# Attention in pairs of heads, with P times V as two fp32 products in the two column halves of TensorE's array and row sums by adds

## The chip, the cores and the metric

The kernel runs on one core of one Trainium2 chip. The metric is the device time of one execution in microseconds, the median of several runs. Three runs of the kernel before gave 4182.15, 4182.94 and 4184.15 us.

## What is computed

Two layers of a hybrid backbone over 256 context tokens and 2,048 latent tokens, 1,024 wide. In each layer one projection feeds three kinds of heads: a bidirectional state-space scan (6 heads), a bidirectional gated DeltaNet (4 heads) and attention (6 query heads, 2 key/value heads of 64 columns). Their outputs are joined and projected back. The change is in the attention:

```python
def _attend(q, k, v):
    ...
    def block(qi):
        s = jnp.einsum('bqhgd,bkhd->bhgqk', qi, k).astype(jnp.float32) * scale
        pr = jax.nn.softmax(s, axis=-1).astype(v.dtype)
        return jnp.einsum('bhgqk,bkhd->bqhgd', pr, v)
```

All is fp32. Head h uses key/value head h // 3. The context tokens attend to themselves in layer 0; in layer 1, the last, only the 2,048 latent tokens are wanted.

## The kernel before

TensorE multiplies in two formats here. `fp32` products are exact enough by themselves; `fp32r` products round their operands, so where precision matters a number is split into a rounded part and a rest, and several fp32r products are added. In the trace an fp32 product leaves two records, an fp32r product one.

Each layer has three parts: the projection, the mixers, the output projection. The mixers run interleaved: DeltaNet preparation (`gdn_pre`, `gdn_solve`), state-space scan (`ssd_states`, `ssd_out`), then the DeltaNet chain (`gdn_chain`), 18 steps of two half steps that each need the one before: products L1094, L1104 and L1114 with copies between them. Attention is written around it as a generator, `attention()`: its first 8 pieces are taken before the chain is written, the rest after. The order on each engine is not that of the text. A scheduler sorts all instructions of the program into one queue per engine by their dependences and its own estimate of their times, so attention fills what the other mixers leave.

Attention is tiled in units. A unit is one head and 512 query columns (24 units in a layer, and 6 small ones of 256 columns in layer 0), over 18 key tiles of 128 rows.

- `unit_max` loads the unit's queries (q2, by DMA on SP's queue; qm, a copy by GpSimd, L522), computes scores for 20 pieces of keys (pq, L531), reduces each to row maxima on VectorE (L533), and turns the negative maxima into a row of qm by four fp32 products with the identity (pm, L541) and a VectorE copy (L542).
- `unit_main` computes for each key tile the transposed scores minus the maximum (pst) by two fp32r products (L562 with khh, L563 with klo and qm), lets ScalarE take the exponential (pe, L565), and multiplies by V into po (L556). V has a column of ones between its two heads (v1, 129 columns), so the product has 65 rows, 64 of values and one of row sums.
- The first 13 units of a layer do this as one fp32 product per key tile. The last 11 split: ScalarE rounds pe to ph (L570), VectorE subtracts to pl (L571), and three fp32r products of ph and pl with the parts of V (vh) replace the fp32 one.
- At a unit's end ScalarE copies po out (L579), and two DMAs store the row sums and the values.

PSUM's eight banks: three for scores (ps_s), one for po, one that every fourth score tile may use before the chain (ps_x), three for the other mixers (four during the chain).

```python
ops = [(v1, pe)] if ph is None else [(vh[0], ph), (vh[1], ph), (vh[0], pl)]
...
nc.tensor.matmul(pst[g * 64:g * 64 + 64, d * 192:(d + 1) * 192], bn[:, g * 64:g * 64 + 64],
                 xd[:, d, 3 * g:3 * g + 3, :], start=True, stop=True)
```

The last two lines are L789 in `ssd_states`: products of 64 output rows that go into the two halves of the partitions in turn. Such a product uses 64 of the array's columns; the trace writes it as 128*64.

## Time and profile before

| | us |
|---|---|
| median of three runs | 4182.94 |
| span of the profiled execution | 4198.6 |
| TensorE busy | 4005.7 (95%) |
| VectorE busy | 2858.0 (68%) |
| ScalarE busy | 1834.2 (44%) |
| GpSimd busy | 1500.3 (36%) |

The profiled execution has no time of its own beside its span, from the first to the last instruction; durations below are its. The attention of layer 0 lies between 711 and 1902 us, that of layer 1 between 2795 and 3991; the rest is projection and output projection. Records of TensorE are longer than the time that a product holds the array, since the next one starts before the last has ended: what a product costs is read from where the next one starts.

### The profile page before, as it was taken

The page shows a single profiled execution, that of the slowest core. Times are in us where ns is not written, and L with a number is a line of the kernel's source. Part 1 is how long each engine was busy: PE and PEld are TensorE (multiplying, and loading weights), DVE is VectorE, ACT ScalarE, POOL GpSimd, SP SyncE. Part 2 cuts the span into 40 slices and gives each one's busy share as a digit, 9 for nine tenths or more (in the row PEclk, how much of TensorE's full clock was granted, in tenths as well). Part 3 has the DMA queues.
Part 4 walks back from the last instruction along what each step waited for, and adds up shares of the span by engine and source line. Part 5 has one row for each costly group of instructions (what it writes and reads, how often), then busy time and mean ns, then how long its engine had stood idle before and what let it go on. Part 6 is the DMA issues. An engine that isn't in the chain of part 4 may idle for free. (4 is left out here: it accounts for less than half of the span.)

```text
span 4198.6 us, 66336 instructions
## 1 busy us (share of the span) xinstructions
PE 4005.7 (95%) x23574; PEld 3044.2 (73%) x23574; DVE 2858.0 (68%) x5652; ACT 1834.2 (44%) x3817; POOL 1500.3 (36%) x1854
## 2 busy tenths in 40 slices
PE   7999999999999999998899999999999999999989
PEld 5899998554566667776678999985545666666667
DVE  6556564889876667875546665648898757677643
ACT  5343432443565545653224434324335645555610
POOL 5121120676465323432313211206755632234300
PEclk9999999999999889999999999999999989898999
DMA  6343432344123333426743434323541233434254
GB/s 198 109 137 103 129 111 93 111 149 165 51 60 89 88 80 83 108 64 214 224 161 118 148 102 128 113 93 103 165 136 55 59 82 77 87 81 97 53 171 155
DMA packets 539143, 477.46 MB, mean 114 GB/s; under 512 B 113784, under 2 KB 476732, under 8 KB 538812
## 3 DMA queue, kind: packets, MB, share of 16 engines
q1 hardware_dynamic: 496956, 437.81, 36.3%
q10 hardware_dynamic: 41856, 35.40, 2.8%
q8 instruction: 187, 3.06, 0.3%
q14 instruction: 144, 1.18, 0.1%
HBM read 328.91 MB, written 144.18 MB: 113 GB/s over the span
## 5 line engine op out<-in xcount | busy, mean ns | idle before, releaser
L565 ACT ACTIVATE pe<-pst 128x512 f32<-128x512 f32 (+1 forms) x876 | 511.7, 594 | 713.7 <-PE pst L563 690.2
L533 DVE TENSOR_REDUCE mx<-pq 128x1 f32<-128x512 f32 (+1 forms) x972 | 594.4, 626 | 135.2 <-PE pq L531 130.8
L531 PE MATMUL pq<-khh,q 128*128 128x512 f32 (+1 forms) x972 | 473.9, 512 | 26.7 <-DVE mx L533 24.8
L556 PE MATMUL po<-pe,v 128*65 128x512 f32 x960 | 487.8, 597 | 1.1 <-ACT os__12118 L579 1.0
L562 PE MATMUL pst<-q,khh 128*128 128x512 f32 (+1 forms) x876 | 433.5, 495 | 16.9 <-DVE mx L533 15.8
L455 PE MATMUL ps<-lo,wh 128*128 128x384 f32 (+2 forms) x1296 | 441.2, 340 | 0.0
L455 PE MATMUL ps<-hi,wl 128*128 128x384 f32 (+2 forms) x1296 | 441.0, 340 | 0.0
L455 PE MATMUL ps<-hi,wh 128*128 128x384 f32 (+2 forms) x1296 | 440.9, 340 | 0.0
L563 PE MATMUL pst<-qm,klo 65*128 65x512 f32 (+1 forms) x876 | 359.1, 411 | 0.0
L401 PE MATMUL ps<-wh,hi 128*128 128x320 f32 (+1 forms) x1120 | 354.3, 318 | 1.9 <-DVE hi L365 1.8
L571 DVE TENSOR_TENSOR pl<-pe,ph 128x512 fp32r<-128x512 f32 x396 | 301.2, 765 | 76.4 <-ACT ph L570 58.6
L401 PE MATMUL ps<-wl,hi 128*128 128x320 f32 (+1 forms) x1120 | 350.3, 314 | 0.0
L401 PE MATMUL ps<-wh,lo 128*128 128x320 f32 (+1 forms) x1120 | 349.7, 315 | 0.7 <-DVE lo L366 0.7
L531 PEld LDWEIGHTS pq<-khh,q 128*128 128x128 f32 x972 | 190.1, 198 | 176.6 <-issue 65.1
L376 DVE TENSOR_TENSOR wl<-wt,wh 128x1024 fp32r<-128x1024 f32 (+3 forms) x144 | 175.8, 1250 | 159.5 <-ACT wh L375 159.3
L556 PE MATMUL po<-ph,vh 128*65 128x512 f32 x792 | 274.7, 429 | 0.6 <-ACT ph L570 0.6
L562 PEld LDWEIGHTS pst<-q,khh 128*128 128x128 f32 x876 | 172.9, 197 | 127.1 <-issue 53.3
L570 ACT CAST ph<-pe 128x512 fp32r<-128x512 f32 x396 | 242.6, 619 | 47.0 <-PE po L556 22.1
L455 PEld LDWEIGHTS ps<-lo,wh 128*128 128x128 f32 x1296 | 244.0, 188 | 10.7 <-issue 0.4
L455 PEld LDWEIGHTS ps<-hi,wl 128*128 128x128 f32 x1296 | 243.4, 188 | 10.4
L455 PEld LDWEIGHTS ps<-hi,wh 128*128 128x128 f32 x1296 | 243.5, 188 | 10.2
L1044 POOL TENSOR_TENSOR wb<-cst,dsc 64x512 f32<-64x512 f32 x72 | 92.8, 1289 | 423.6 <-issue 225.1
(585 smaller groups left out, 8849.4 us busy)
## 6 DMA issues: line engine op xcount, KB each, us to landing
wt<-in_w_in_dram SPq DMA_DIRECT2D x72, 512.0 KB
acv<-pre_d SPq DMA_DIRECT2D x68, 512.0 KB
wmt<-in_w_mod_dram SPq DMA_DIRECT2D x48, 512.0 KB
pre_d<-pre SPq DMA_DIRECT2D x34, 512.0 KB
kqc<-kt_d SPq DMA_DIRECT2D x68, 256.0 KB
wt<-in_w_in_dram SPq DMA_DIRECT2D x24, 668.0 KB
wt<-in_w_in_dram SPq DMA_DIRECT2D x24, 640.0 KB
q<-qt_d SPq DMA_DIRECT2D x48, 256.0 KB
```

What stands on the lines that cost most here:

```text
L376: nc.vector.tensor_tensor(out=wl[:, ks, :], in0=wt, in1=wh[:, ks, :].bitcast(F32), op=ALU.subtract)
L401: nc.tensor.matmul(ps, hh[:, k, a], ww[:, k, :], start=(n == 0), stop=(n == 3 * KD - 1))
L455: nc.tensor.matmul(ps, ww[:, k, m * P:(m + 1) * P], hh[:, k, s0:s0 + sn], start=(n == 0), stop=(n == 3 * KD - 1))
L531: nc.tensor.matmul(pq[:, :n], q2[:, u * P:(u + 1) * P], khh[:, kvh, k0t * P + a:k0t * P + a + n], start=True, stop=True)
L533: nc.vector.tensor_reduce(mx[:, i:i + 1], pq[:, :n], axis=AX.X, op=ALU.max)
L556: nc.tensor.matmul(po[0:65, :qn], v[:, kt, vs], p[:, :qn], start=(kt == k0t and j == 0), stop=(kt == k1t - 1 and j == len(ops) - 1))
L562: nc.tensor.matmul(pt[:, :qn], khh[:, kvh, ks], q2[:, :qn], start=True, stop=False)
L563: nc.tensor.matmul(pt[:, :qn], klo[:, kvh, ks], qm[:, :qn], start=False, stop=True)
L565: nc.scalar.activation(out=pe[:, :qn], in_=pt[:, :qn], func=AF.Exp, scale=0.125)
L570: nc.scalar.copy(out=ph, in_=pe)
L571: nc.vector.tensor_tensor(out=pl, in0=pe, in1=ph.bitcast(F32), op=ALU.subtract)
L1044: nc.gpsimd.tensor_tensor(out=wb[dk[d], d, :, :, cS[d]].rearrange("p c h n -> p (c h) n"), in0=cc("ident")[dk[d], None, dk[d]].to_broadcas ...
```

## The change

Units become pairs of heads: 12 of 512 columns in a layer, 3 small ones in layer 0. `v1` loses its column of ones. For each key tile the scores of both heads go into one `pe` of 1,024 columns (five buffers, before four of 512), and P times V is one fp32 product per head, 64 rows each, into partitions 0 to 63 and 64 to 127 of po. No unit splits the exponentials any more. Row sums are made apart, in a bank pl of their own: in the first four pairs of a layer and in the small ones ("P") by fp32 products with a matrix of ones, also in halves; in the other eight pairs GpSimd ("G", 14 of 18 tiles) and VectorE ("V", 4 of 18) add the tiles up, and two products per engine and pair finish the sum. P times V runs three tiles behind the scores, two tiles at a time. The maxima are turned by fp32r products of 65 rows and copied by ScalarE; qm's other rows come by DMA. ps_x is gone, pl takes its bank, and the chain has three banks instead of four. Four pieces of attention, each of two heads, are written before the chain.

```diff
-        v1 = kv.tile([P, NT, 129], F32, name="v1")
+        v1 = kv.tile([P, NT, P], F32, name="v1")
...
-                    if g == 0 and bi == 3:
-                        nc.gpsimd.tensor_copy(v1[:, :, 64:65], cc("ones")[:, None, 0:1].to_broadcast([P, NT, 1]))
...
-                                    nc.vector.tensor_copy(v1[:, t, 0:64], ps[:, 192:256])
-                                    nc.vector.tensor_copy(v1[:, t, 65:129], ps[:, 256:320])
+                                    nc.vector.tensor_copy(v1[:, t, :], ps[:, 192:320])
...
-                psg[2] += 1
-                if psg[0] and psg[2] > 60 and psg[2] % 4 == 0:
-                    return psg[0].tile([P, 512], F32, name=name, tag="x")
                 return ps_s.tile([P, 512], F32, name=name, tag="s")
 
-            banks(1, 3)
-
-            def unit_max(h, q0, qn, k0t, k1t, st):
-                kvh = h // 3
-                q2 = ap_.tile([P, 512], F32R, name="q2", bufs=3)
+            banks(0, 3)
+
+            nmz = apz.tile([P, 2, 4, 65], F32R, name="nmz")
+            nc.gpsimd.memset(nmz.bitcast(F32), 0.0)
+
+            def unit_max(pr, q0, qn, k0t, k1t, st):
+                h0, nu = 2 * pr, qn // P
+                q2 = ap_.tile([P, 2, 512], F32R, name="q2", bufs=3)
+                qm = ap_.tile([65, 2, 512], F32R, name="qm", bufs=3)
                 with tc.high_priority():
-                    nc.sync.dma_start(q2[:, :qn].bitcast(F32), qt_d[:, h, q0:q0 + qn])
-                qm = ap_.tile([65, 512], F32R, name="qm", bufs=3)
-                nc.gpsimd.tensor_copy(qm[0:64, :qn], q2[0:64, :qn].bitcast(F32))
+                    nc.sync.dma_start(q2[:, :, :qn].bitcast(F32), qt_d[:, h0:h0 + 2, q0:q0 + qn])
+                    nc.sync.dma_start(qm[0:64, :, :qn].bitcast(F32), qt_d[0:64, h0:h0 + 2, q0:q0 + qn])
                 st.update(q2=q2, qm=qm)
                 kn = (k1t - k0t) * P
                 pieces = [(a, min(512, kn - a)) for a in range(0, kn, 512)]
-                nm = ap_.tile([P, 4], F32, name="nm")
-                for u in range(qn // P):
-                    mx = ap_.tile([P, 8], F32, name="mx", bufs=4)
-                    for i, (a, n) in enumerate(pieces):
-                        pq = aslot("pq")
-                        nc.tensor.matmul(pq[:, :n], q2[:, u * P:(u + 1) * P], khh[:, kvh, k0t * P + a:k0t * P + a + n],
-                                         start=True, stop=True)
-                        nc.vector.tensor_reduce(mx[:, i:i + 1], pq[:, :n], axis=AX.X, op=ALU.max)
-                        yield
-                    nc.vector.tensor_reduce(nm[:, u:u + 1], mx[:, 0:len(pieces)], axis=AX.X, op=ALU.max)
-                nc.vector.tensor_scalar(out=nm[:, :qn // P], in0=nm[:, :qn // P], scalar1=-1.0, scalar2=None, op0=ALU.mult)
+                mx = ap_.tile([P, 2, 4, 5], F32, name="mx")
+                for j in range(2):
+                    kvh = (h0 + j) // 3
+                    for u in range(nu):
+                        for i, (a, n) in enumerate(pieces):
+                            pq = aslot("pq")
+                            nc.tensor.matmul(pq[:, :n], q2[:, j, u * P:(u + 1) * P], khh[:, kvh, k0t * P + a:k0t * P + a + n],
+                                             start=True, stop=True)
+                            nc.vector.tensor_reduce(mx[:, j, u, i:i + 1], pq[:, :n], axis=AX.X, op=ALU.max)
+                            yield
+                for j in range(2):
+                    nc.vector.tensor_reduce(nmz[:, j, 0:nu, 64:65], mx[:, j, 0:nu, 0:len(pieces)], axis=AX.X, op=ALU.max, negate=True)
                 for _ in range(3):
                     yield
-                pm = aslot("pm")
-                for u in range(qn // P):
-                    nc.tensor.matmul(pm[64:65, u * P:(u + 1) * P], nm[:, u:u + 1], ident, start=True, stop=True)
-                nc.vector.tensor_copy(qm[64:65, :qn], pm[64:65, :qn])
+                for j in range(2):
+                    pm = aslot("pm")
+                    for u in range(nu):
+                        nc.tensor.matmul(pm[0:65, u * P:(u + 1) * P], nmz[:, j, u, :], identr, start=True, stop=True)
+                    nc.scalar.copy(out=qm[64:65, j, :qn], in_=pm[64:65, :qn])
                 yield
 
-            def unit_main(h, q0, qn, k0t, k1t, st, sp=()):
-                kvh = h // 3
+            def unit_main(pr, q0, qn, k0t, k1t, st, how):
+                h0 = 2 * pr
+                kvh = (h0 // 3, (h0 + 1) // 3)
                 q2, qm = st["q2"], st["qm"]
                 po = ps_o.tile([P, 512], F32, name="po", tag="po")
-                pend = []
+                pl = ps_o.tile([P, 512], F32, name="pl", tag="pl")
+                ones = cc("ones")[:, 0:64]
+                half = (slice(0, 64), slice(64, 128))
+                pend, held, acc = [], {}, {}
+                plan = [how(kt - k0t) for kt in range(k0t, k1t)]
+                n_pl = plan.count("P") + len({e for e in plan if e != "P"})
+                done = [0]
+
+                def sums(src):
+                    for j in range(2):
+                        nc.tensor.matmul(pl[half[j], :qn], ones, src[:, j, :qn], start=(done[0] == 0), stop=(done[0] == n_pl - 1))
+                    done[0] += 1
 
                 def pv():
-                    kt, pe, ph, pl = pend.pop(0)
-                    vs = slice(kvh * 64, kvh * 64 + 65)
-                    ops = [(v1, pe)] if ph is None else [(vh[0], ph), (vh[1], ph), (vh[0], pl)]
-                    for j, (v, p) in enumerate(ops):
-                        nc.tensor.matmul(po[0:65, :qn], v[:, kt, vs], p[:, :qn], start=(kt == k0t and j == 0),
-                                         stop=(kt == k1t - 1 and j == len(ops) - 1))
+                    kt, pe = pend.pop(0)
+                    for j in range(2):
+                        nc.tensor.matmul(po[half[j], :qn], v1[:, kt, kvh[j] * 64:kvh[j] * 64 + 64], pe[:, j, :qn],
+                                         start=(kt == k0t), stop=(kt == k1t - 1))
+                    if plan[kt - k0t] == "P":
+                        sums(pe)
 
                 for kt in range(k0t, k1t):
                     ks = slice(kt * P, (kt + 1) * P)
-                    pt = aslot("pst")
-                    nc.tensor.matmul(pt[:, :qn], khh[:, kvh, ks], q2[:, :qn], start=True, stop=False)
-                    nc.tensor.matmul(pt[:, :qn], klo[:, kvh, ks], qm[:, :qn], start=False, stop=True)
-                    pe = ap_.tile([P, 512], F32, name="pe", bufs=4)
-                    nc.scalar.activation(out=pe[:, :qn], in_=pt[:, :qn], func=AF.Exp, scale=0.125)
-                    ph = pl = None
-                    if kt in sp:
-                        ph = spl.tile([P, 512], F32R, name="ph", bufs=2)
-                        pl = spl.tile([P, 512], F32R, name="pl", bufs=2)
-                        nc.scalar.copy(out=ph, in_=pe)
-                        nc.vector.tensor_tensor(out=pl, in0=pe, in1=ph.bitcast(F32), op=ALU.subtract)
-                    pend.append((kt, pe, ph, pl))
-                    if len(pend) > (3 if sp else 1):
+                    pe = ap_.tile([P, 2, 512], F32, name="pe", bufs=5)
+                    for j in range(2):
+                        pt = aslot("pst")
+                        nc.tensor.matmul(pt[:, :qn], khh[:, kvh[j], ks], q2[:, j, :qn], start=True, stop=False)
+                        nc.tensor.matmul(pt[:, :qn], klo[:, kvh[j], ks], qm[:, j, :qn], start=False, stop=True)
+                        nc.scalar.activation(out=pe[:, j, :qn], in_=pt[:, :qn], func=AF.Exp, scale=0.125)
+                    e = plan[kt - k0t]
+                    if e != "P":
+                        eng = nc.gpsimd if e == "G" else nc.vector
+                        if e in acc:
+                            eng.tensor_tensor(out=acc[e][:, :, :qn], in0=acc[e][:, :, :qn], in1=pe[:, :, :qn], op=ALU.add)
+                        elif e in held:
+                            acc[e] = ap_.tile([P, 2, 512], F32, name="acc" + e, bufs=1)
+                            eng.tensor_tensor(out=acc[e][:, :, :qn], in0=held[e][:, :, :qn], in1=pe[:, :, :qn], op=ALU.add)
+                        else:
+                            held[e] = pe
+                    pend.append((kt, pe))
+                    if len(pend) >= 4:
+                        pv()
                         pv()
                     yield
                 while pend:
                     pv()
-                os_ = ap_.tile([65, 512], F32, name="os_", bufs=1)
-                nc.scalar.copy(out=os_[:, :qn], in_=po[0:65, :qn])
-                ob, sb_ = (0, 64) if kvh == 0 else (1, 0)
-                nc.sync.dma_start(sm_d[None, HQ * q0 + h * qn:HQ * q0 + (h + 1) * qn], os_[sb_:sb_ + 1, :qn])
-                nc.sync.dma_start(mx_d[640 + h * 64:704 + h * 64, q0:q0 + qn], os_[ob:ob + 64, :qn])
+                for e in held:
+                    sums(acc.get(e, held[e]))
+                os_ = ap_.tile([P, 512], F32, name="os_", bufs=1)
+                nc.scalar.copy(out=os_[:, :qn], in_=po[:, :qn])
+                sm_ = ap_.tile([65, 512], F32, name="sm_", bufs=1)
+                nc.scalar.copy(out=sm_[:, :qn], in_=pl[0:65, :qn])
+                for j in range(2):
+                    f0 = HQ * q0 + (h0 + j) * qn
+                    nc.sync.dma_start(sm_d[None, f0:f0 + qn], sm_[64 * j:64 * j + 1, :qn])
+                nc.sync.dma_start(mx_d[640 + h0 * 64:768 + h0 * 64, q0:q0 + qn], os_[:, :qn])
                 yield
...
+                def early(k):
+                    return "P"
+
+                def late(k):
+                    return "V" if k % 4 == 3 else "G"
...
-                    if i == 13:
-                        for _ in range(2):
-                            vh.append(spl.tile([P, NT, 129], F32R, name=f"vh{len(vh)}", bufs=1))
-                        nc.scalar.copy(out=vh[0], in_=v1)
-                        nc.vector.tensor_tensor(out=vh[1], in0=v1, in1=vh[0].bitcast(F32), op=ALU.subtract)
-                    spn = () if i < 13 else range(NT)
                     nxt = ms[i:i + 1] + mb[i + 1:i + 2]
-                    left = (21 + 3) * (i + 1 < len(big)) + 3 * (i < len(small))
+                    left = 43 * (i + 1 < len(big)) + 7 * (i < len(small))
                     done = 0
-                    for j, _ in enumerate(unit_main(*un, sb[i], spn)):
-                        want = left * (j + 1) // (NT - 4)
+                    for j, _ in enumerate(unit_main(*un, sb[i], early if i < 4 else late)):
+                        want = left * (j + 1) // (NT - 2)
                         adv(nxt, want - done)
                         done = max(done, want)
                     adv(nxt, 99)
                     if i < len(small):
-                        for _ in unit_main(*small[i], ss_[i]):
+                        for _ in unit_main(*small[i], ss_[i], early):
                             pass
-                    if i >= 14:
-                        next(side_work, None)
...
-            for _ in range(8):
+            for _ in range(4):
                 next(att)
-            banks(0, 4)
+            banks(0, 3)
             gdn_chain(rq)
```

The scheduler sorts the queues anew. Two places on TensorE's queue show what becomes of the pairs; the rows name product and operands (pq scores for the maxima, pst transposed scores, po the output, pl the sums; the size is that of the output).

In layer 0, beside the DeltaNet preparation, the kernel before (L556 is P times V, L531 the scores for the maxima):

```order
L556 MATMUL po_11202<-pe_11258,v1_352 65x512
L531 MATMUL pq_11273<-khh_350,q2_11246 128x512
L531 MATMUL pq_11276<-khh_350,q2_11246 128x256
L556 MATMUL po_11202<-pe_11270,v1_352 65x512
L531 MATMUL pq_11287<-khh_350,q2_11246 128x512
L934 MATMUL ptv_7374<-cst_63,kv__7318 128x128
```

The same stage of the changed kernel (L564 is P times V, L558 the sums, L528 the scores for the maxima, L969 DeltaNet preparation):

```order
L528 MATMUL pq_11139<-khh_350,q2_11067 128x512
L564 MATMUL po_11011<-pe_11119,v1_352 64x512
L558 MATMUL pl_11012<-pe_11119,cst_63 64x512
L969 MATMUL pg_7597<-kq_7529 64x128 x4
L969 MATMUL pg_7604<-kq_7529 64x128 x4
L528 MATMUL pq_11142<-khh_350,q2_11067 128x256
L564 MATMUL po_11011<-pe_11119,v1_352 64x512
L558 MATMUL pl_11012<-pe_11119,cst_63 64x512
```

The two halves that read one pe no longer follow each other: between L564 and L558 of the first head and those of the second stand products of other shapes, and each L558 follows the L564 of its own half.

In layer 0, beside the chain, the kernel before, with a split head (L556 three times per tile, L562 and L563 transposed scores):

```order
L556 MATMUL po_18197<-ph_18304,vh0_16670 65x512
L556 MATMUL po_18197<-ph_18304,vh1_16671 65x512
L531 MATMUL pq_18331<-khh_350,q2_18207 128x512
L562 MATMUL pst_18334<-q2_17900,khh_350 128x512
L563 MATMUL pst_18334<-qm_17902,klo_351 128x512
L531 MATMUL pq_18346<-khh_350,q2_18207 128x512
L556 MATMUL po_18197<-pl_18305,vh0_16670 65x512
L556 MATMUL po_18197<-ph_18324,vh0_16670 65x512
L556 MATMUL po_18197<-ph_18324,vh1_16671 65x512
```

The changed kernel beside the chain (L1116, L1126 and L1090 are chain and its preparation, L574 and L575 transposed scores):

```order
L564 MATMUL po_17929<-pe_17951,v1_352 64x512
L1116 MATMUL p_13937<-Z0_13855,kqc_13726 64x64 x4
L564 MATMUL po_17929<-pe_17951,v1_352 64x512
L1090 MATMUL pv_13897<-xf0_12743,vt_13914 32x32 x16
L1116 MATMUL p_13937<-Z1_13860,kqc_13726 64x64 x4
L574 MATMUL pst_17976<-q2_17560,khh_350 128x512
L575 MATMUL pst_17976<-qm_17561,klo_351 128x512
L528 MATMUL pq_17981<-khh_350,q2_17940 128x512
L564 MATMUL po_17929<-pe_17971,v1_352 64x512
L528 MATMUL pq_17984<-khh_350,q2_17940 128x512
L1126 MATMUL p_13950<-r0_13946,xf1_12744 64x64 x4
```

Here too one product of the chain or of the scores stands between the two L564 of one pe.

## Rows read from the trace of the kernel before

**Rows 1.** Page, sections 1 and 2: busy time of TensorE; its granted clock in 40 slices.

```profile
PE 4005.7 (95%) x23574; PEld 3044.2 (73%) x23574; DVE 2858.0 (68%) x5652; ACT 1834.2 (44%) x3817; POOL 1500.3 (36%) x1854
PEclk9999999999999889999999999999999989898999
```

**Rows 2.** Windows of the attention, layer 0 then 1, before and beside the chain.

```profile
core 0: us, PE busy (x) PEld busy (x) DVE busy (x) ACT busy (x) POOL busy (x), PEclk, DMA share, GB/s
711.00:1340.00 629.00, 594.09 (x2766) 345.37 (x2765) 520.59 (x1144) 297.52 (x739) 389.53 (x510) 0.99 0.34 102
1340.00:1902.00 562.00, 542.40 (x4166) 393.54 (x4163) 403.37 (x758) 311.79 (x609) 198.04 (x170) 0.91 0.38 87
2795.00:3395.00 600.00, 571.42 (x2661) 339.30 (x2660) 497.44 (x1095) 278.77 (x680) 362.23 (x472) 0.98 0.32 99
3395.00:3991.00 596.00, 565.46 (x4225) 403.93 (x4222) 407.04 (x758) 317.11 (x618) 187.13 (x172) 0.89 0.38 81
```

**Rows 3.** Groups by shape: TensorE, VectorE, ScalarE and GpSimd (busy, mean | idle before).

```profile
L556 PE MATMUL po<-pe,v 128*65 128x512 f32 x936 | 481.5, 603 | 1.1 <-ACT os__12118 L579 1.0
L556 PE MATMUL po<-ph,vh 128*65 128x512 f32 x792 | 274.7, 429 | 0.6 <-ACT ph L570 0.6
L541 PE MATMUL pm<-cst,nm 128*1 128x128 f32 x408 | 56.6, 283 | 5.1 <-DVE nm L536 3.5 <-DVE zn L420 1.6
L571 DVE TENSOR_TENSOR pl<-pe,ph 128x512 fp32r<-128x512 f32 x396 | 301.2, 765 | 76.4 <-ACT ph L570 58.6 <-PE po L556 13.0 <-ACT Z L1106 1.7
L565 ACT ACTIVATE pe<-pst 128x512 f32<-128x512 f32 x864 | 507.5, 597 | 710.6 <-PE pst L563 687.3 <-PE po L556 15.2 <-DVE pl L571 1.2
L217 POOL TENSOR_TENSOR wml<-wmt,wmh 128x1024 fp32r<-128x1024 f32 x24 | 62.9, 2636 | 55.3 <-ACT wmh L214 55.1
L981 POOL TENSOR_TENSOR M<-N,B 128x1024 f32<-128x1024 f32 x4 | 8.0, 1990 | 14.4 <-DMA B<-be_d 7.4 <-DMA cd_d<-pre 7.0
```

**Rows 4.** Timeline of TensorE, whole heads with fp32 P times V: start, length, instructions.

```profile
1005.90 1.02 PE L556 MATMUL po<-pe,v 128*65 128x512 f32 x2
1006.36 1.03 PE L531 MATMUL pq<-khh,q 128*128 128x512 f32 x2
1007.23 0.39 PE L562 MATMUL pst<-q,khh 128*128 128x512 f32 x1
```

**Rows 5.** Timeline of TensorE, head with split exponentials.

```profile
1671.64 0.40 PE L556 MATMUL po<-pl,vh 128*65 128x512 f32 x1
1671.87 0.62 PE L556 MATMUL po<-ph,vh 128*65 128x512 f32 x2
1672.33 0.40 PE L562 MATMUL pst<-q,khh 128*128 128x512 f32 x1
```

**Rows 6.** Timeline of TensorE where the used part of the array changes.

```profile
1642.32 0.50 PE L562 MATMUL pst<-q,khh 128*128 128x512 f32 x1
1642.66 0.41 PE L563 MATMUL pst<-qm,klo 65*128 65x512 f32 x1
...
1655.20 0.39 PE L563 MATMUL pst<-qm,klo 65*128 65x512 f32 x1
1655.52 0.96 PE L1104 MATMUL p<-r,xf 64*64 64x64 f32 x16
```

**Rows 7.** Timeline of TensorE, products of 192 columns: four records, then two.

```profile
1001.42 0.55 PE L789 MATMUL pst<-xd,bn 128*64 128x192 f32 x4
1001.89 0.64 PE L556 MATMUL po<-pe,v 128*65 128x512 f32 x1
...
3233.39 0.49 PE L843 MATMUL po<-S,bc 64*128 64x192 f32 x2
3233.81 0.44 PE L835 MATMUL pd<-rr,sufr 128*128 128x384 f32 x1
```

**Rows 8.** Waits of TensorE, 711 to 1340 us.

```profile
PE pst L562 <- DVE mx L533: 10.2, 13, 2.1
PE pq L531 <- DVE mx L533: 8.7, 9, 3.7
```

14 lines of the change are left out of this document (8 added, 6 removed).

## The prediction

> **What bounds the kernel now.** I read the page first: TensorE is busy for 95% of the span, and its clock is granted nearly whole [rows 1]. Then the windows, to see the stages that the change touches. In both layers attention runs in two stretches: beside the state-space and DeltaNet preparation (711 to 1340 us, 2795 to 3395), then beside the DeltaNet chain (1340 to 1902, 3395 to 3991). TensorE is busy for 94 to 97% of each, VectorE for at most 83%, ScalarE for 55%, GpSimd for 62% [rows 2]. So what counts is TensorE's time. Busy time is no price, since records overlap (a mean of 603 ns for one of the two records of an fp32 product [rows 3]). I price by starts in the timeline.
>
> - An fp32 product of 512 columns: from 1005.90 to 1007.23 stand one product P times V (two records) and two fp32r products. An fp32r product takes 0.23 us (1671.64 to 1671.87 [rows 5]). 1.33 - 0.47 = **0.86 us** [rows 4].
> - A split tile: 0.46 us for two products and 0.23 for the third, **0.70 us** [rows 5]. Nearly the price of one fp32 product, so giving up the split gains little by itself.
>
> The change must therefore win by running two fp32 products in one product's time. Do column halves overlap? The kernel has such a place: L789 puts products of 192 columns alternately into the halves. Four records, two products, take 0.47 us until the next line starts; the two records of one product of that length take 0.42 [rows 7]. So two halves **that follow each other directly** do run side by side. Whether they follow each other is the order's to say.
>
> **The change, part by part.**
>
> *P times V and row sums.* On TensorE's queue the changed kernel has 876 half-width products at L564 and 364 at L558, 1,240 in all, 24 of them 256 columns wide. The pairs are written next to each other, but the queue has them apart: pst and pq products, 128 columns wide, stand between the halves. I counted along the queue how many products find the other half as direct neighbour: 90. So 1,150 turns of the array remain where 620 were meant. At 0.86 us: 989, less 24 x 0.43 = 10 for the narrow ones: 979 us. Before: 468 wide fp32 products x 0.86 and 12 narrow ones x 0.43 make 408 us, 396 split tiles x 0.70 make 277. **+294 us.** A lone half costs as much as a whole array: the rate per column is the same for 192 columns in a half, above, as for 512 of 65.
>
> *Changes of the used part.* Between a product that uses 128 columns and one that uses 64 the array does not stream on. Going in takes 0.32 us where 0.23 is normal (1655.20 to 1655.52 [rows 6]): 0.09. The first wide product after a narrow stretch takes 0.34 (1642.32 to 1642.66): 0.10 more. Inside and on leaving: two passes of 192 columns stream for 0.86 x 192/512 = 0.32 us, and L789 takes 0.47 to 0.48: 0.16 more [rows 7]. 0.35 for a visit, or 0.17 for one change. Both queues have many already, in the chain's 64x64 products and in L541's single-column ones. Counted along the queues by shape, there are 1,242 changes before and 2,445 after; 1,203 x 0.17 = **+205 us.**
>
> *The row of maxima.* L541's 204 fp32 products of 128 columns (408 records [rows 3]) become fp32r at L539: 204 x 0.86 x 128/512 = 44 us become 204 x 0.23/4 = 12. **-32 us.** Scores and maxima (L562, L563, L531) keep their numbers: 0.
>
> Sum on TensorE: 294 + 205 - 32 = **+467 us** at full clock. Most of it falls in the stretches beside the preparation, which were granted 0.98 and 0.99, a little beside the chain (0.91 and 0.89) [rows 2]; at 0.97 it is 481.
>
> *What stops covering.* TensorE waited 19 us in the first stretch for VectorE to empty a slot [rows 8]. With TensorE slower, VectorE is ahead; I take back 15 us a layer, **-30**. Against it, attention now ends before the chain: 144 of the chain's 576 first products (L1116) stand behind the last attention row, 18 of its 72 half steps. A half step takes 562/36 = 15.6 us now [rows 2], with attention in it: 1,177 fp32r products and 40 rows of maxima stand on the queue in that stretch, 279 us, 307 at its clock. That leaves 7.1 us for a half step's own products, changes and waits. Alone it may wait for its copies where attention filled in: between 0 and 8.5 us more for each of 18. I take 1.8, near the low end because the 7.1 already hold waits, **+32**; the ends are 0 and +153.
>
> *Other engines, at nothing.* 396 casts leave ScalarE and 396 subtractions (765 ns) VectorE [rows 3]; neither bounds, so that gains nothing beyond the 30 above. 16 late pairs bring 13 adds each to GpSimd and 3 to VectorE. No GpSimd add of 128x1024 fp32 is in the trace; the nearest are 1,990 and 2,636 ns [rows 3], so 26 to 34 us a pair. The same pair holds TensorE for 72 x 0.23 (scores) + 40 x 0.23 (maxima) + 40 x 0.86, 60 us even without changes, and GpSimd is 62% busy at most: covered, if its queue does not come late. VectorE's 48 adds cost less than its 396 subtractions did. ScalarE's new copies (two maxima rows, one more result per pair) are some 0.6 us each on an engine half idle. The qm rows come by DMA instead of GpSimd: 27 more transfers on SP's queue, with a DMA share of 0.32 to 0.38. One PSUM bank less for scores early, three instead of four for the chain: 0, with an upper bound of some 20 us a layer, doubling the waits of [rows 8]. v1's copies in the projection: two become one, off the path.
>
> Together 481 - 30 + 32 = **+483 us**. The profiled span, 4198.6 us, becomes 4682; it stands 15.7 above the median of the plain runs, so I say 4183 + 483, some **4665 us**.
>
> **The rivals.**
>
> *Changes cost nothing (chance 0.12).* A narrow product of 512 columns may hide the weight load and emptying that products of 64 and 192 show. For it: my price comes from short products. Against it: the first wide product after is 512 long and still takes 0.34 [rows 6]. Then 262/0.97 - 30 + 32 = +272: **4455 us**.
>
> *The clock falls (0.12).* Beside the chain, where narrow products and waits are many, 0.89 to 0.91 was granted, not 0.98 [rows 2]; that is stretches at 1.2 instead of 2.4 GHz. Now the earlier stretches are full of narrow products too. They grow to some 1,830 us for both layers; at 0.90 that is 9% more, +165: **4830 us**. Against it: fp32 products of 65 columns held 0.99 before.
>
> *GpSimd holds the exponentials (0.08).* pe has five buffers, and one is free only when the add has read it. GpSimd's queue is in order; an add behind the chain's weight products, or behind a wait for a DMA, comes late, exp waits for a buffer and TensorE for exp. One such hold of 6 us, three adds, in each of 16 pairs: +100, **4765 us**. It decides as soon as GpSimd falls more than four tiles behind.
>
> *The halves overlap after all (0.06): faster.* The mechanism is that halves of a pair share one turn of the array although other products stand between them in the queue. Then 620 turns: 533 - 5 = 528, against 685 now, and 32 saved: -189 us. With the changes at half price, -86; with the clock and the chain's tail, -90: **4095 us**. It needs more than some 540 of the 620 pairs to overlap before it pays for the changes. For it: L789's halves overlap [rows 7]. Against it: they are neighbours in the queue, and here 90 are. The Trainium skill, page TensorEngine Tiling (Array Packing), section Theoretical Speedup, speaks for it: a dimension of at most 64 gives up to twice the speed, and by that alone P times V and the sums would take the 528 us. The Trainium skill, page TensorE: Matmul & The Clock Gate, Part 3, speaks against it: products start and end in program order, with no reordering. No row here shows a half overlapping across a wide product.
>
> **How the numbers follow.** 0.62 for the forecast as priced, 0.12 + 0.12 + 0.08 for the slower rivals, 0.06 for the faster one. The range goes from the case without a price for changes to the case with the lower clock and some of the tail's upper bound: **4455 to 4870 us**, which leaves out the faster case and about a seventh of the rest. Faster by over 0.2% (what a measurement of this kernel can tell from no change, some 8 us) 0.06, within it 0.01, slower 0.93.
>
> **What would show it.** Right: L564 groups of one or two records with pst and pq between them, 0.86 us apart from their neighbour's start plus the change; the stretch before the chain longer by some 300 us a layer, since 926 of the 1,240 half products stand ahead of the chain, the one beside it shorter by some 40; TensorE the busy engine in both; the end of attention before the chain's end. Wrong: L564 rows of both halves with nearly the same start throughout; or long waits of TensorE for exp with GpSimd busy; or a chain tail of over 100 us a layer. If L564 stands alone but its visit takes well under 1.2 us, the price of a change was wrong.

## The result and the profile after

| | before | after |
|---|---|---|
| median, us | 4183.55 (4 runs) | 4680.95 (4 runs, 4678.85 to 4684.12) |
| span of the profiled execution, us | 4198.6 | 4678.6 |
| TensorE busy, us | 4005.7 | 4481.5 |
| mean granted clock | 0.958 | 0.954 |

The changed kernel is slower: its time is 1.1165 times that of before, 95% interval 1.1121 to 1.1208. The forecast was 4665 us. The span grew by 480.0 us and TensorE's busy time by 475.8, so the loss is TensorE's, as [rows 1] had it. The page of the changed kernel, busy time and granted clock:

```profile
PE 4481.5 (96%) x23702; PEld 2983.3 (64%) x23702; DVE 2658.6 (57%) x5008; ACT 1616.5 (35%) x3473; POOL 1939.6 (41%) x2008
...
PEclk9999998999999999976999999989999999999679
```

Its groups by shape, P times V and the sums (busy us, mean ns of a record | idle before), beside [rows 3]:

```profile
L564 PE MATMUL po<-pe,v 128*64 128x512 f32 x1728 | 886.5, 626 | 0.0
...
L558 PE MATMUL pl<-pe,cst 128*64 128x512 f32 x576 | 288.4, 593 | 0.0
```

The other engines lie well below TensorE. The clock is low in the slices in which the chain runs alone at the end of each layer's mixers. The same stages as in [rows 2], as windows (columns: window, length, busy time of PE, PEld, DVE, ACT, POOL, granted clock, DMA share, GB/s). For each layer: first transposed score to first chain product, then to the last P times V, then to the end of the chain.

```profile
738.00:1643.00 905.00, 887.96 (x3416) 403.68 (x3415) 568.67 (x1119) 336.15 (x804) 507.10 (x541) 0.99 0.25 73
1643.00:2020.00 377.00, 375.98 (x2716) 210.82 (x2715) 186.48 (x308) 132.61 (x280) 221.76 (x139) 0.99 0.38 85
2020.00:2163.00 143.00, 115.28 (x866) 91.62 (x867) 71.66 (x131) 40.56 (x83) 86.46 (x75) 0.56 0.66 169
...
3091.00:3954.00 863.00, 849.12 (x3232) 382.01 (x3234) 541.21 (x1055) 314.90 (x737) 478.89 (x517) 0.99 0.24 70
3954.00:4347.00 393.00, 392.03 (x2782) 216.22 (x2781) 186.29 (x311) 134.83 (x283) 224.81 (x138) 0.97 0.36 82
4347.00:4469.00 122.00, 93.71 (x784) 83.69 (x783) 49.84 (x109) 26.72 (x67) 61.40 (x63) 0.55 0.47 109
```

Where the 480 us lie, with the same marks in both traces (the start is that of the kernel, in layer 1 the end of layer 0's mixers; the mixers end with the last product of attention or chain):

| | layer 0 | layer 1 |
|---|---|---|
| start to the first transposed score | +29 | +25 |
| to the first chain product | +263 | +258 |
| to the end of the mixers | -35 | -62 |

The two layers sum to 478, and the output projection adds the rest. The loss sits in the stretch ahead of the chain, where TensorE is busy for 888 of 905 us. Beside the chain the time fell although TensorE was busier than before. Behind the last P times V the chain has 143 and 122 us left, at about half the clock; behind the last row sum, which ends at 2034.3 and 4367.2 us, it runs alone for 129 and 102. The last row sum of layer 0 and the first of the ten half steps behind it:

```profile
2032.42 1.92 PE L558 MATMUL pl<-accV,cst 128*64 128x512 f32 x4
...
2039.99 1.28 PE L1116 MATMUL p<-Z,kqc 64*64 64x64 f32 x13
```

What one visit of the array's half costs is in the timeline (start, length, instruction):

```profile
1008.84 1.07 PE L564 MATMUL po<-pe,v 128*64 128x512 f32 x2
1009.75 1.02 PE L558 MATMUL pl<-pe,cst 128*64 128x512 f32 x2
1010.70 0.50 PE L528 MATMUL pq<-khh,q 128*128 128x512 f32 x1
1011.13 0.64 PE L564 MATMUL po<-pe,v 128*64 128x512 f32 x1
```

A half product, a half product of sums and one wide fp32r product take from 1008.84 to 1011.13, 2.29 us. At the plain rates of 0.86, 0.86 and 0.23 they would take 1.95. The visit costs 0.34 us more, the prediction's two changes at 0.17. Both half products belong to one head and so to the same half of the array; the other head's follow behind wide products.

### The profile page after: what moved, and what is told of

It is laid out like the page before. It is cut to its first block, busy times and chain, and to the rows that moved or that the text cites. A ratio compares the mean times of both kernels' runs of the same rounds, so it can differ in the third digit from the quotient of the medians.

```text
span 4678.6 us, 65132 instructions
## 1 busy us (share of the span) xinstructions
PE 4481.5 (96%) x23702; PEld 2983.3 (64%) x23702; DVE 2658.6 (57%) x5008; ACT 1616.5 (35%) x3473; POOL 1939.6 (41%) x2008
## 5 line engine op out<-in xcount | busy, mean ns | idle before, releaser
L564 PE MATMUL po<-pe,v 128*64 128x512 f32 x1752 | 892.1, 622 | 0.0
L576 ACT ACTIVATE pe<-pst 128x512 f32<-128x512 f32 x876 | 496.2, 593 | 1069.5 <-PE pst L575 1063.1
L581 POOL TENSOR_TENSOR accG<-accG,pe 128x1024 f32<-128x1024 f32 x192 | 459.6, 2394 | 263.4 <-ACT pe L576 261.1
L528 PE MATMUL pq<-khh,q 128*128 128x512 f32 (+1 forms) x972 | 407.2, 455 | 25.8 <-DVE mx L530 12.3
L574 PE MATMUL pst<-q,khh 128*128 128x512 f32 x876 | 405.2, 463 | 15.9 <-DVE mx L530 14.0
L574 PEld LDWEIGHTS pst<-q,khh 128*128 128x128 f32 x876 | 165.6, 189 | 328.0 <-issue 106.8
L528 PEld LDWEIGHTS pq<-khh,q 128*128 128x128 f32 x972 | 181.6, 197 | 297.5 <-issue 106.3
L575 PE MATMUL pst<-qm,klo 65*128 65x512 f32 x876 | 347.4, 397 | 0.0
L564 PEld LDWEIGHTS po<-pe,v 128*64 128x64 f32 x1752 | 161.0, 136 | 230.8 <-issue 211.5
L558 PE MATMUL pl<-pe,cst 128*64 128x512 f32 x600 | 293.8, 585 | 0.0
L1245 PE MATMUL psd<-woh,mh 128*128 128x512 f32 x544 | 215.5, 398 | 31.2 <-ACT mh L1236 29.0
```

The lines of the kernel that those rows point to most:

```text
L528: nc.tensor.matmul(pq[:, :n], q2[:, j, u * P:(u + 1) * P], khh[:, kvh, k0t * P + a:k0t * P + a + n], start=True, stop=True)
L558: nc.tensor.matmul(pl[half[j], :qn], ones, src[:, j, :qn], start=(done[0] == 0), stop=(done[0] == n_pl - 1))
L564: nc.tensor.matmul(po[half[j], :qn], v1[:, kt, kvh[j] * 64:kvh[j] * 64 + 64], pe[:, j, :qn], start=(kt == k0t), stop=(kt == k1t - 1))
L574: nc.tensor.matmul(pt[:, :qn], khh[:, kvh[j], ks], q2[:, j, :qn], start=True, stop=False)
L575: nc.tensor.matmul(pt[:, :qn], klo[:, kvh[j], ks], qm[:, j, :qn], start=False, stop=True)
L576: nc.scalar.activation(out=pe[:, j, :qn], in_=pt[:, :qn], func=AF.Exp, scale=0.125)
```

## The experiments

Twelve kernels ran. Two theories were put first. **A**: TensorE's work adds up wherever it stands. **B**: beside the chain the chain keeps a pace of its own, so only work ahead of it counts.

### e1_pairs: the two halves as direct neighbours

```diff
+ def pair(mm):
+     mm(1)
+     with tc.high_priority():
+         tc.keep_in_program_order(mm(0))
- for j in range(2):
-     nc.tensor.matmul(po[half[j], :qn], ...)
+ pair(lambda j: nc.tensor.matmul(po[half[j], :qn], ...))
```

The sums (pl) are issued in the same way.

> The second product of each pair is tied to the place right behind the first, nothing else changes. On TensorE's queue 1,240 half products then take 620 turns instead of 1,150, and the used part of the array changes 1,783 times instead of 2,445. Theory A (TensorE's work adds up in both stretches, as the prediction had it): 530 x 0.86 + 662 x 0.17 = 569 us less, 4112 us, faster than the kernel before. Theory B (beside the chain the pace is the chain's own, 14 to 15 us for a half step with or without attention, so only what stands ahead of the chain counts): ahead of the chain 882 turns become 458 and 1,499 changes 1,017, 365 + 82 = 447 us less, 4234 us. Rival C (halves overlap anyway, or the loss has another cause): 4680 us, no change.

Measured: 4405.13 us (ratio to before 1.0502, 1.0458 to 1.0547), 276 less than the changed kernel. The timeline shows two products, four records, where one stood:

```profile
1008.68 1.08 PE L568 MATMUL po<-pe,v 128*64 128x512 f32 x4
1009.59 1.03 PE L563 MATMUL pl<-pe,cst 128*64 128x512 f32 x4
1010.55 0.50 PE L578 MATMUL pst<-q,khh 128*128 128x512 f32 x1
```

From 1008.68 to 1009.59 are 0.91 us for two halves; above, 0.91 us held one. Halves overlap here when they are direct neighbours; with other products between them each held the array for a time of its own. In the groups the products of P times V and the sums fall from 886.5 + 288.4 to these:

```profile
L568 PE MATMUL po<-pe,v 128*64 128x512 f32 x1728 | 513.7, 676 | 0.2 <-ACT pe L580 0.2
...
L563 PE MATMUL pl<-pe,cst 128*64 128x512 f32 x576 | 152.1, 607 | 0.3 <-ACT sm__11894 L603 0.3
```

That is 509 us less, and still only 276 are gained. The prices hold roughly: busy time multiplied by the mean granted clock, a rough measure of the work, fell by some 528 us (4481.5 x 0.954 less 4122.2 x 0.909), near the 569 of theory A. Two things keep the time from following. The windows, cut at the same three marks (layer 0):

```profile
741.00:1530.00 789.00, 727.05 (x3416) 373.90 (x3415) 585.62 (x1121) 340.30 (x806) 502.88 (x540) 0.94 0.28 83
1530.00:1890.00 360.00, 352.79 (x2603) 223.24 (x2599) 181.05 (x298) 130.12 (x270) 216.03 (x134) 0.85 0.37 85
1890.00:2041.00 151.00, 123.60 (x985) 98.95 (x984) 71.24 (x140) 44.12 (x91) 92.45 (x82) 0.57 0.69 175
```

First, the chain's stretch did not shorten: 360 + 151 = 511 us against 377 + 143 = 520, as B says. Ahead of it 116 us are gained. Second, the granted clock fell, from 0.99 to 0.94 ahead and 0.85 beside. TensorE is idle for 62 us of the 789, mostly waiting for VectorE's maxima, where it was idle for 17 of 905. One place where the clock falls (in brackets the idle time before):

```profile
1134.26 0.50 PE L578 MATMUL pst<-q,khh 128*128 128x512 f32 x1
1134.60 0.40 PE L579 MATMUL pst<-qm,klo 65*128 65x512 f32 x1
1137.17 0.79 PE L578 MATMUL pst<-q,khh 128*128 128x512 f32 x1 [2.16 <-DVE mx L530]
1137.76 0.63 PE L579 MATMUL pst<-qm,klo 65*128 65x512 f32 x1
```

Before the wait the step from L578 to L579 takes 0.34 us, behind it 0.59: the engine is at 1.2 GHz, here until about 1161. B's direction holds, its amount does not: both theories left the clock at its height.

### e2_later, e3_all_late, e4_early_start: the same work elsewhere

e2 holds the maxima of the sixth and later units back until the chain's first product (a dependence of order alone); e3 takes the row sums of all large pairs by adds; e4 gives q2 and mx tiles of their own, allocated ahead of the others.

```diff
# e2_later, in unit_max
+ if gated and j + u + i == 0:
+     behind(mm)
...
# e3_all_late, in attention
- unit_main(*un, sb[i], early if i < 4 else late)
+ unit_main(*un, sb[i], late)
# e4_early_start, in unit_max
- q2 = ap_.tile([P, 2, 512], F32R, name="q2", bufs=3)
+ q2 = apq.tile([P, 2, 512], F32R, name="q2", bufs=3)
...
```

> The changed kernel, halves apart as they are (1,162 turns, 2,464 changes), but the sixth pair of each layer and those after it may not start before the chain's first product. It only moves attention: ahead of the chain 584 turns are left of 882, 840 changes of 1,499 and 1,020 score products of 1,945; behind the chain now stand 230 turns, 434 changes and 600 score products. Theory A: the work is the same, only the chain's lonely end goes, 4640 to 4660 us. Theory B: 256 + 112 + 213 = 581 us less ahead, 198 + 74 + 138 = 410 more behind, up to 80 more beside the chain: 4510 to 4590 us.

> All large pairs sum their rows by adds on GpSimd and VectorE; 256 products of the sums go (1,150 turns become 900, 2,445 changes 2,289). The scheduler then puts all attention of a layer ahead of the chain (1,945 score products there become 2,724, changes 1,499 become 2,001, turns 882 become 900), and all 72 half steps of the chain stand alone. Theory A: 215 + 27 us less, some 100 more for lonely half steps, 4540 us. Theory B: the chain's stretches keep their 515 to 520 us, ahead of them 15 + 179 + 85 = 279 us more: 4960 us, if GpSimd keeps up with the adds.

> The changed kernel with q2 and mx in a pool of their own that is allocated first; nothing else changes. In the trace of the changed kernel the first scores of a layer wait until the projection has ended, where the kernel before had its first 20 maxima done during it; from the end of the projection to the first transposed score it is some 30 us more in each layer. On the queue the first score product now stands some 870 places earlier. Theory A: 60 us less, some 20 more for lonely half steps: 4640 us. Theory B: 60 us less, but 38 turns, 83 changes and 145 score products more ahead of the chain, 33 + 14 + 33 = 80 more: 4700 us. If the late start has nothing to do with where the tiles lie: first scores as late as before.

Measured (one run each): 4851.47, 5010.29 and 4704.76 us. e3 and e4 came out near B, e2 well above both. e4 starts its scores 24 us earlier and reaches the chain 54 us later, because more attention now goes ahead of it: what the early start gains is given back. In e3 all attention goes ahead of the chain, and the chain runs alone:

```profile
1925.00:2330.00 405.00, 320.95 (x2832) 298.59 (x2831) 141.36 (x293) 75.43 (x198) 162.67 (x153) 0.50 0.48 105
```

405 us for 36 half steps are 11.2 us each, at half the clock. In the changed kernel 26 half steps lie beside attention in layer 0, from 1642.7 to 2040.0 us, with TensorE busy throughout until the last P times V; one took 15.3. Attention beside the chain goes with some 4 us more a half step.

e2 shows a third bound. Its windows, from the first score; the second begins where the units ahead are done:

```profile
742.00:1229.00 487.00, 481.42 (x1891) 205.99 (x1889) 288.62 (x638) 145.72 (x318) 203.16 (x301) 1.00 0.30 94
1229.00:1492.00 263.00, 180.29 (x690) 147.72 (x690) 147.04 (x293) 100.06 (x320) 169.13 (x185) 0.53 0.22 58
1492.00:2040.00 548.00, 546.64 (x3819) 308.45 (x3818) 304.35 (x520) 187.96 (x397) 318.11 (x218) 0.98 0.38 88
2040.00:2260.00 220.00, 205.16 (x565) 72.58 (x564) 79.88 (x112) 77.01 (x131) 98.35 (x45) 0.98 0.09 30
```

Among its waits from 1229 to 1492 us (total, times, longest) the first is:

```profile
PE pt L899 <- DVE t L892: 64.9, 18, 7.2
```

For 263 us the preparation of the chain runs without attention; TensorE waits for VectorE for 64.9 of them, at about half the clock. The units held back then reach 220 us past the chain. Theory **C**: the preparation is a bound of its own ahead of the chain, and what is taken from there below that bound saves nothing. What stands alone there is the stage `ssd_out`; e11 below comes back to it.

### e5_wide: no change of the used part

```diff
- nc.tensor.matmul(po[half[j], :qn], v1[:, kt, kvh[j] * 64:kvh[j] * 64 + 64], pe[:, j, :qn], ...)
+ nc.tensor.matmul(po[:, :qn], v1[:, kt, :], pe[:, j, :qn], ...)
```

The sums are widened in the same way, with all 128 columns of the ones.

> The same 1,240 half products are written 128 columns wide (all 128 columns of v1 or of the ones as weights), so that they no longer change the used part of the array; their number and rows stay. po and pl then hold the two heads of a pair added up, so the output is not the attention's. The queue on TensorE has 1,022 changes of the used part instead of 2,445. Theory A (each change costs about 0.17 us of TensorE, as in the prediction's sum): TensorE's busy time falls from 4,481 to about 4,240 us (1,423 x 0.17 = 242) and the time to 4,400 to 4,480. Rival (the changes cost nothing, the halves alone are the loss): busy time stays at 4,450 to 4,500 and the time at 4,600 to 4,690.

Measured: 4566.37 us (2 runs, ratio 1.085, 1.0788 to 1.0912), TensorE busy 4348.2. That is between the two, 133 us of busy time less and not 242. The unit price, though, is plain in the timeline:

```profile
1083.17 1.02 PE L564 MATMUL po<-pe,v 128*128 128x512 f32 x2
1084.03 1.02 PE L558 MATMUL pl<-pe,cst 128*128 128x512 f32 x2
1084.48 0.80 PE L574 MATMUL pst<-q,khh 128*128 128x512 f32 x1
1085.12 0.40 PE L575 MATMUL pst<-qm,klo 65*128 65x512 f32 x1
```

The same three products take from 1083.17 to 1085.12: 1.95 us, the sum of the plain rates, where the visit in the halves took 2.29. The price is that of the used part, not of fp32 beside fp32r. The expectation forgot that 90 pairs of the changed kernel do share a turn, and none does when wide: by that price 90 x 0.86 = 77 us come back. 242 - 77 = 165 us, nearer to the 133; the rest was not traced.

### e6 to e8: pairs, started early and held back

```diff
# e6_pairs_early: e1_pairs and e4_early_start together
# e7_pairs_gate9: also the hold of e2_later, from the ninth unit
+ mb = [unit_max(*un, st, i >= 8) for i, (un, st) in enumerate(zip(big, sb))]
# e8_pairs_gate8: from the eighth
+ mb = [unit_max(*un, st, i >= 7) for i, (un, st) in enumerate(zip(big, sb))]
```

> e1_pairs and e4_early_start together: the two halves of a product as direct neighbours, and q2 and mx in tiles of their own, so that the first scores need not wait for the projections. Theory B (only what lies ahead of the chain's first product counts, beside it the chain keeps its own pace of 14 to 15 us per half step): the earlier start brings more attention ahead of the chain (500 half products instead of 480 in the first layer), so the gain of up to 25 us per layer is given back as it was with the halves apart: 4,390 to 4,425. Theory A (TensorE's work adds up): the start 25 us earlier in each layer counts: 4,350 to 4,375.

> e6_pairs_early, and the maxima of the ninth and later units may not start ahead of the chain's first product. The queue then has 434 half products and 864 score products ahead of the chain in the first layer (e1_pairs: 480 and 1,002), 410 and 828 in the second (436 and 922); the others go beside the chain, whose last half steps without attention go from 5 and 4 to 1. The number of products stays. Theory B: the stretch ahead shrinks by 23 pairs x 1.17 + 138 x 0.45 = 89 us in the first layer and 57 in the second, the chain's stretch stays at 510 to 520 us, and the early start now counts: 4,405 less 146 less 0 to 50: 4,210 to 4,260. Theory A: 4,350 to 4,405. Theory C (the chain's preparation on VectorE and ScalarE is the bound ahead, as where the sixth unit was held back): 4,350 or more, with TensorE idle in the last part of the stretch ahead.

> As e7_pairs_gate9, with the eighth and later units held back: 394 half products and 752 score products ahead of the chain, 44 and 62 behind its end. Theory B: the stretch ahead shrinks by another 20 pairs x 1.17 + 112 x 0.45 = 74 us per layer, and 22 pairs x 0.91 + 62 x 0.25 = about 36 us come behind the chain: another 30 to 40 us per layer, 4,140 to 4,190. Theory C: the preparation becomes the bound, the last part of the stretch ahead stands with TensorE idle and at the low clock, and the time is 4,230 or more.

Measured: 4437.02 (4424.87 to 4473.81), 4412.80 (4393.60 to 4433.44) and 4484.56 us (4464.51 to 4516.51). A falls with e6: the earlier start gains nothing, and the time lies 12 us above B's range. B's price for work ahead falls with e7 and e8, where C holds. The last part of the stretch ahead in e7:

```profile
1390.00:1502.00 112.00, 71.26 (x300) 58.79 (x301) 53.98 (x107) 35.95 (x116) 68.45 (x77) 0.50 0.29 69
```

No attention is left there; TensorE does 71 us of preparation in 112 at half the clock, and in e8 such a piece begins 100 us earlier.

### e9 and e10: more adds or none

```diff
# e9_gate9_adds: e7_pairs_gate9, and
- unit_main(*un, sb[i], early if i < 4 else late)
+ unit_main(*un, sb[i], late)
# e10_pairs_all_sums: e1_pairs, and
- unit_main(*un, sb[i], early if i < 4 else late)
+ unit_main(*un, sb[i], early)
```

> e7_pairs_gate9 with the row sums of the first four units of a layer by adds on GpSimd and VectorE too, as those of the later units are: 128 products in pairs fewer, all ahead of the chain (306 half products there in the first layer instead of 434, as many beside it). Theory B (TensorE's work ahead of the chain sets that stretch): 64 pairs x 1.17 = 75 us less per layer, 4,250 to 4,290. Theory C (with units held back, the chain's preparation is the bound there, and TensorE idles at its end): TensorE's idle time ahead grows by what its work loses, 4,390 to 4,440; more if the adds hold GpSimd, on which the preparation waits.

> e1_pairs with every row sum as a product in pairs on TensorE, none by adds: 512 half products more (256 pairs x 0.86 = 220 us of TensorE). The scheduler then puts less ahead of the chain: 794 score products instead of 1,002 and as many half products (480), 336 half products beside it instead of 152, and 44 behind its end (first layer); nothing is held back by hand. Theory A (TensorE's work adds up): 4,560 to 4,640. Theory B (only work ahead of the chain and behind it counts, the chain keeps a pace of 14 to 15 us per half step beside any of this): ahead 208 x 0.45 = 94 us less per layer, the chain's stretch 510 to 540 us, about 30 to 60 us of attention behind it: 4,310 to 4,420. Theory C (the preparation bounds the stretch ahead): 4,420 to 4,500, with TensorE idle there.

Measured: e9 4745.18 us (ratio 1.1283, 1.1196 to 1.1369), e10 4306.34 (1.0265, 1.0217 to 1.0313). The two go opposite ways, both against the count of products: e9 has 256 half products fewer than e7 and takes 332 us more; e10 has 512 more than e1 and takes 99 less. e9 lies above all its ranges, so that only C's last clause, adds that hold GpSimd, is left of them; e10 lies 4 us below B's range. The windows of e10, to the chain's first product and to its end, in both layers:

```profile
738.00:1394.00 656.00, 622.64 (x3167) 326.34 (x3166) 474.93 (x1031) 295.16 (x728) 375.39 (x487) 0.98 0.34 101
1394.00:1923.00 529.00, 522.21 (x4140) 316.38 (x4141) 244.37 (x488) 187.27 (x396) 160.30 (x153) 0.96 0.38 88
...
3515.00:4038.00 523.00, 507.31 (x4067) 305.30 (x4066) 242.25 (x473) 176.00 (x373) 154.76 (x145) 0.94 0.38 86
```

The stretch ahead is 656 us, 14 more than before the change, at a clock of 0.98, and the chain's stretch (529) took in more than twice the half products of e1 for 18 us more. On TensorE's queue 794 score products stand ahead of the chain in layer 0; the kernel before has 794 there as well, e1 1,002 and the changed kernel 996. So with the adds the scheduler puts some 200 more of them ahead. In e9 the stretch ahead is 930 us (715 to 1645), though TensorE has less to do; the adds took 203.5 us of GpSimd there, and TensorE stood idle for 215 us:

```profile
715.00:1645.00 930.00, 715.17 (x2956) 404.96 (x2957) 625.79 (x1100) 322.39 (x779) 605.89 (x586) 0.75 0.24 71
```

The group of GpSimd's adds in the same stretch:

```profile
L593 POOL TENSOR_TENSOR accG<-accG,pe 128x1024 f32<-128x1024 f32 x84 | 203.5, 2423 | 69.7 <-ACT pe L588 69.0
```

Which part of this the adds cost through GpSimd's queue, and which through VectorE's, was not separated.

### e11 and e12: adds beside the chain alone

```diff
# e11_adds_from_8th: e10_pairs_all_sums, and
- unit_main(*un, sb[i], early)
+ unit_main(*un, sb[i], early if i < 7 else late)
# e12_early_adds_from_9th: i < 8, and q2 and mx as in e4_early_start
```

> e10_pairs_all_sums, with the adds kept for the eighth to the twelfth unit of a layer alone, which all run beside the chain (there GpSimd was busy for 160 of 529 us). 160 pairs of sums fewer on TensorE; ahead of the chain 480 half products and 794 score products as in e10 in the first layer (452 and 749 in the second, e10: 484 and 777), beside it 236 instead of 336, behind it 12 instead of 44. Theory B: the stretch ahead stays (about 25 us less in the second layer), the chain's stretch stays at its own pace of 520 us, and the 52 and 75 us of attention behind it shrink to about 10 to 25 each: 4,180 to 4,230. Theory D (adds on GpSimd and VectorE lengthen whatever stretch they lie in, as ahead in e9): the chain's stretch grows by 40 us or more per layer, 4,280 or more.

> e10_pairs_all_sums with the adds kept from the ninth unit on, and with q2 and mx in tiles of their own for the earlier start. Ahead of the chain 508 half products and 836 score products (e10: 480 and 794) in the first layer, 480 and 798 in the second (484 and 777); beside it about 250; 4 half products behind it. Theory B: first scores 25 us earlier in each layer, 14 x 1.0 + 42 x 0.45 = 33 us more ahead in the first and about 8 in the second, 40 to 60 us less behind the chain in each: 4,306 - 50 + 41 - 105 = 4,190, so 4,170 to 4,230. Theory D: the chain's stretch grows by 40 us or more per layer, 4,260 or more.

Measured: 4327.31 us (1.0303, 1.0241 to 1.0365) and 4283.82 (1.0205, 1.0146 to 1.0263). Both times are D's, but only e12 has 40 us more in the chain's stretch of both layers (55 and 42 more than e10). e11 in layer 0 and in the chain's stretch of layer 1:

```profile
738.00:1394.00 656.00, 621.53 (x3156) 324.45 (x3155) 473.48 (x1029) 294.34 (x727) 374.57 (x485) 0.98 0.33 96
1394.00:1936.00 542.00, 522.31 (x3983) 322.40 (x3981) 304.53 (x503) 202.42 (x423) 320.29 (x219) 0.90 0.37 86
1936.00:1976.00 40.00, 14.94 (x39) 3.25 (x38) 17.81 (x22) 14.05 (x19) 11.05 (x9) 0.59 0.74 232
...
3499.00:4065.00 566.00, 547.46 (x3913) 341.24 (x3909) 284.72 (x491) 193.90 (x405) 298.73 (x204) 0.83 0.34 79
```

The stretch ahead equals e10's. That separates the adds: those of the fifth to seventh units, which e1 has and e11 has not, go with 789 against 656 us ahead. Most of the 133 us, 126, lie in one stage. `ssd_out` is a row of 18 steps with work on all engines, and L861 is one of its products. The group of L861 with its first and last start in layer 0, in e1 and in e10, and the same product in e2 (L864), where no attention was left beside it:

```profile
L861 PE MATMUL pd<-rr,sufr x72: 334/340/667, 1125.4 to 1496.4; 128*128 128x384 f32 x72
...
L861 PE MATMUL pd<-rr,sufr x72: 333/338/445, 1118.4 to 1363.6; 128*128 128x384 f32 x72
...
L864 PE MATMUL pd<-rr,sufr x72: 336/522/687, 1220.7 to 1459.6; 128*128 128x384 f32 x72
```

The stage begins 384 us after the first transposed score in e1 and 380 in e10, and then takes 371 and 245 us. From that product's first to its last start, its length follows the time of GpSimd's adds in it more closely than the attention beside it or the clock (the four runs left out fit in):

| layer 0, us | `ssd_out` | GpSimd's adds in it | score products in it | granted clock |
|---|---|---|---|---|
| before | 238 | 0 | 241 | 1.00 |
| e2 | 239 | 0 | 0 | 0.54 |
| e10 | 245 | 0 | 228 | 0.99 |
| e9 | 264 | 0 | 0 | 0.51 |
| e5 | 283 | 38 | 240 | 0.98 |
| e8 | 297 | 47 | 153 | 0.69 |
| e7 | 323 | 78 | 265 | 0.81 |
| e1 | 371 | 118 | 419 | 0.90 |
| changed kernel | 379 | 114 | 410 | 0.99 |
| e3 | 386 | 93 | 283 | 0.88 |

So this stage, too, has a pace of its own, some 240 us, and the adds that lie in it lengthen it by at least their time on GpSimd; the longer it lasts, the more attention the scheduler puts into it, ahead of the chain. VectorE's adds in it are few (11 in e1), and no run moved GpSimd's adds alone, so that this rests on the table.

Beside the chain the adds go with 13 and 43 us more (529 and 523 in e10), at a lower clock; D's 40 us showed in one layer of e11 only. What e10 had behind the chain was hardly a loss: it covered the wait for the last results, in which e11 does little for 40 us, and e10's output projection started at 1946 us, e11's at 1976. By its median e12 is the fastest version found, though its interval and e10's overlap; both lie above 1.

## Why the prediction was right

The time came out at 4680.95 against 4665 us, the span at +480.0 against +483. Step by step:

- **What bounds.** Right: TensorE is busy for 475.8 of the 480.0 us more.
- **1,150 turns at 0.86 us.** Right. Halves that are no neighbours do not overlap (2.29 us for the visit above), neighbours do (0.91 for two in e1). The rival that the halves overlap after all falls; its some 540 pairs are 467 / 0.86 and leave out the 90 that are neighbours already; with these it is 633, over the 620 there are, as long as all changes are paid. The Trainium skill, page TensorEngine Tiling (Array Packing), section Theoretical Speedup, gives up to twice the speed for a dimension of at most 64; here e1 shows it for direct neighbours, and the changed kernel shows none of it for the others.
- **0.17 us for a change.** Right: 2.29 against 1.95 us in e5 is 0.34 for the two changes of a visit. The rival in which they cost nothing falls. That the whole 205 us were paid was not measured by itself; e5 moves other things too.
- **The row of maxima, -32.** Its busy time fell from 56.6 us [rows 3] to 23.0, in line.
- **Waits given back, -30.** Right in size, not all by the waits named: in layer 0 those for maxima ahead of the chain fell from the 19 us of [rows 8] to 11, but TensorE's idle time there fell from 35 us [rows 2] to 17, and in layer 1 from 29 to 14.
- **The chain's tail, +32.** This step failed, and the sign named for it showed, a tail of over 100 us a layer (129 and 102). The sum priced a half step alone at 7.1 + 1.8 = 8.9 us; the 10 and 8 of the tail, from 2040.0 to 2163.6 and from 4378.1 to 4468.8 us, took 12.4 and 11.3, at a clock of about 0.55, and e3 puts a half step without any attention at 11.2. By these, 18 half steps cost 86 us over 18 x 7.1 and not 32. The 7.1 came from taking attention's work at a clock of 0.91 off the 15.6, as if that work were additive and the clock would stay. The half steps beside attention took 15.3 and 15.2 us, about as before (15.1 and 15.7 to the chain's end). To the end of the mixers the chain's stretch still shrank by 35 and 62 us, near the forecast 40: the tail's half steps are shorter than those beside attention, and before the change attention ran 13 us past the chain.
- **The late start.** Not foreseen: the first transposed score comes 29 and 25 us later. It stands 37 us behind the projection's last product in both layers; before, it began with that product. e4 shows that taking it away alone gains nothing.
- **The stretch ahead, some +300 a layer.** 263 and 258 came, from 452 and 430 turns, 502 and 500 more changes and some 200 more score products that stood ahead. The last were counted, but their cause was not seen. The forecast of some 600 us for both layers was 79 too high, and the late start, which the sum did not have, added 54: that the total came within 16 us is in part luck.
- **The adds, at nothing.** One took 2394 ns, inside the 1,990 to 2,636 of [rows 3], and TensorE did not wait for them. ScalarE's exponentials waited for TensorE's scores (1063.1 us in all) and 2.0 us for an add, so the rival that GpSimd holds them falls. But nothing was most likely too low a price: GpSimd's adds lie among the steps of `ssd_out`. With pairs those of the middle units go with 133 us more ahead of the chain in layer 0 (e1 against e11). In the changed kernel `ssd_out` is 141 us longer than before, with 114 us of adds in it; TensorE is busy there for 367 of 380 us, with attention that in e10 ran beside the chain. What the changed kernel would gain without its adds was not tried.
- **The clock falls ahead of the chain.** Not in the changed kernel: 0.99. It fell in e1 (0.94), where TensorE had less to do and more waits.

So the change loses by its halves standing apart (276 us when mended, against a clock that falls), by adds (99 us more when all go), most likely those in `ssd_out`, and by what is left, 111 us against before in e10. In the profiled executions e10 is 98 us longer: 29 and 60 us lie ahead of the first transposed score of each layer (counted in layer 1 from the first product of layer 0's output projection), 14 and 9 between it and the chain, and from the chain on it is 14 us shorter. So a later start is most of it, and the changes of the used part, 1,836 instead of 1,242 on the queue, show little.

## What to carry to other kernels

Count in the queue, not in the text, how many column halves find their other half as direct neighbour, and charge each visit for its two changes, before trusting a factor of two. Ask of each stretch which engine or chain ends it: work moved to where a serial chain sets the pace was nearly free here, while work taken from a stretch whose other bound stood close behind saved nothing. Adds moved to an engine that is half idle can still lengthen a serial stage that uses the same engine, and the scheduler then fills that stage with work that was cheaper elsewhere.

## What the hardware showed beyond that

- Less work can cost clock. With the halves in pairs TensorE did 359 us less in busy time, and its mean granted clock fell from 0.954 to 0.909; a record of the transposed scores' first product then lasted 489 ns instead of 463. In e10, with 220 us of paired products more, it was 0.969.
- fp32 products of the full width among fp32r products have no extra price (1.95 us for the three of e5, the sum of their plain rates); the price came with the narrower part alone.
- The chain alone ran at half the clock and was yet faster per half step (11.2 us in e3) than beside attention at 0.99 (15.3).
- A serial stage that gives work to several engines in turn can be almost blind to TensorE's clock: `ssd_out` took 239 us alone at 0.54 (264 at 0.51 in e9) and 238 us beside attention at 1.00.
